# Gated delta rule: the inverse of the next pair of heads beside the recurrence of this one, TensorE in order of emission

## The chip, the cores and the metric

The kernel runs on one core of a Trainium2 chip. The metric is the device time in microseconds of one execution: 2815.87 us, the median of three runs (2814.72 to 2819.11).

## The reference

A chain of decoder blocks over 512 tokens of width 1024 in float32: a gated feed-forward, a block of parallel mixers, a cross attention, a feed-forward, a second block with retention and sparse attention, a third with neighbourhood and latent attention, a last feed-forward. The change lies in the parallel mixers of the first block, in one of the two mixers above all, the gated delta rule with 8 heads of 128, in chunks:

```python
m = jnp.where(strict, einsum(kb, kc) * decay, 0.0)        # per head and chunk
t_sys = eye + m
u = triangular_solve(t_sys, vb)
w = triangular_solve(t_sys, kb * exp(gc))
a_qk = einsum(qc, kc) * decay
def step(state, xs):                                      # over the chunks
    v_new = u_i - w_i @ state
    o_i = (q_i * exp(g_i)) @ state + a_i @ v_new
    state = state * exp(g_last) + k_dec.T @ v_new
```

q, k and v come from one projection each, a causal convolution of 4 taps and SiLU; q and k are normalised by their length. The result of a head is normalised, multiplied by SiLU of a projection z, and projected. The other mixer multiplies a projection by the sigmoid of another and convolves it with 31 taps.

## The kernel before

The kernel is written on a framework that tracks what each instruction needs, and that plans the order of every engine's instructions when the program is built: by a priority that falls in the order of emission, by what is ready, and by its own estimate of durations. `tc.high_priority(-n)` puts instructions n places later. The order that a queue then has is fixed; each engine takes its instructions in that order, and waits where one is not ready.

A projection of 128 features (`glu_conv`, `gdn_rows`, `gate_proj`, and the z product in `gdn_head`) loads a block of 1024 by 128 weights (`wload`, L273): one DMA of 512 KB in SyncE's queue (L277) into one of two raw buffers, a rounded copy `wh` by ScalarE (L270), the remainder `wl` by an engine named in `now["lo"]`, here GpSimd (L271). Then 24 products (`mm3`, L196, lines 198 to 200) of 128x512 add up in one PSUM bank of the group `pj`, which has three.

The gated delta rule uses chunks of 128 tokens, four to a head. For a head, `gdn_rows` (L692) makes k, q and v, takes the four taps (L716), turns them on TensorE (L726), squares them (L731), sums the rows (L734, L738), scales k (L740), and turns k back (L744). `gdn_decay` (L757) builds the decay, from a row that is loaded to all partitions, and the two score products of a chunk (L773) with their evictions (L776, L778); it stores one of them to `sm` in DRAM (L779). `gdn_blocks` (L783) inverts the 16x16 diagonal blocks of two heads at once on VectorE: it loads them (L790), does 15 steps of two dependent operations (L796, L798), stores the result and its transpose (L799, L802), and loads both back as Y and X (L804, L806). `gdn_head` (L814) completes the inverse from blocks of 16 to 128 by products in three levels (L822; eight steps), and then goes through the four chunks, three steps each (products with the state and the gating, L858; with the inverse, L866; with the new rows, L872). Each of these steps is one round of evictions by VectorE or ScalarE, after which comes the generator's `yield`. It ends with the norm, the z projection and the product with it (L886 to L910).

`glu_conv` (L561) makes two projections; ScalarE's sigmoid of one (L578) is multiplied with the other's bank by VectorE into `pad` (L579; two buffers), and 31 taps follow, the first on ScalarE, 30 on VectorE (L585), into the only bank of the group `cv`.

The stage is set together at L1821 to L1825: first a few projections; then two streams are emitted side by side by `interleave` (L212), which always advances the one with the smaller sum of estimated TensorE time (`pe_ns`, from `mm` and `mm3`) by its weight. The first holds the rows of heads 2 to 7, the convolutions and the `ga` gate; the second the pairs of heads, one after another, each as decay, blocks, heads (`gdn_pair`, L809). TensorE's order is the planner's.

Of the kernel before, what the change touches and what calls it, by code (L numbers as in the profile page):

```python
# [2 lines left out]

# [14 lines left out]
T = 512  # L18
# [7 lines left out]
CONV_LATER = 150  # L26
# [82 lines left out]
def kernel(ctx: ExitStack, tc: tile.TileContext, a: dict, out: bass.AP, upto=99):  # L109
# [9 lines left out]
    ypool = ctx.enter_context(tc.tile_pool(name="ypool", bufs=7))  # L119
# [9 lines left out]
    now = {"lo": V, ("sb", "wr"): (rpool, 2), ("sb", "wh"): (wpool, 4), ("sb", "wl"): (wpool, 4)}  # L129
# [94 lines left out]

# [48 lines left out]
    def wload(src, k0, kn, c0, cn, eng=None):  # L273
# [3 lines left out]
        S.dma_start(rv, src[k0 * 128:(k0 + kn) * 128, c0:c0 + cn].rearrange("(k p) c -> p k c", p=128))  # L277
# [32 lines left out]
    def feature_proj(src, c0, nf, act, nk, consume, tag="pj", group=2):  # L310

        f = 0
        while f < nf:
# [3 lines left out]
            for k0 in range(0, nk, step):  # L317
# [7 lines left out]
                yield  # L325
# [3 lines left out]
            yield  # L329
# [231 lines left out]
    def glu_conv(c0, c1):  # L561
        w = dram_w("w_in")
        act = acts["b1_1"]
        for c in range(c0, c1):
# [3 lines left out]
            for base in (4112, 4112 + 1024):  # L568
                p = bank()
                h, l = wload(w, 0, 8, base + c * 128, 128)  # L570
                for k in range(8):
                    mm3(p, (h[:, k], l[:, k]), (act.hi(k), act.lo(k)), k == 0, k == 7)
                ps.append(p)
                yield
            pad = work("pad", (128, T + 30))
            V.memset(pad[:, :30], 0.0)
            sg = work("sg", (128, T))
            A.activation(sg, ps[1], AF.Sigmoid)  # L578
            V.tensor_mul(pad[:, 30:], sg, ps[0])  # L579
# [6 lines left out]
            yield  # L586
# [40 lines left out]
    def gdn_gates():  # L627
# [7 lines left out]
        ab = work("sg", (128, T))  # L635
# [4 lines left out]
        small = work("gsmall", (128, 12, 32))  # L640
# [34 lines left out]
        V.tensor_tensor(small[:, 8], pc[:, 32:64], small[:, 5], OP.subtract)  # L675
        A.activation(small[:, 6], small[:, 5], AF.Exp)
        V.tensor_scalar(small[:, 7], small[:, 6], -1.0, None, OP.mult)
        V.tensor_scalar(small[:, 11], small[:, 5], -1.0, None, OP.mult)
        A.activation(small[:, 8], small[:, 8], AF.Exp)
        A.activation(small[:, 9], pc[:, 32:64], AF.Exp)  # L680
        gd.update(rq=sm(10), beta=sm(0), ngc=sm(11), egc=sm(6), negc=sm(7), kd=sm(8), egl=sm(9))
# [10 lines left out]
    def gdn_rows(h):  # L692
# [7 lines left out]
        for i in (1, 0, 2):  # L700
            if ("pre", h) in gd:
                p = gd["pre", h][i]
            else:
                hw, lw = wload(w, 0, 8, i * 1024 + h * 128, 128)
                p = bank()
                for k in range(8):
                    mm3(p, (hw[:, k], lw[:, k]), (act.hi(k), act.lo(k)), k == 0, k == 7)
            x = work("xr", (128, T))
# [14 lines left out]
            yield  # L723
            p = tbank()
            for c in range(4):
                PE.transpose(p[:, c], xf[:, c], ident)  # L726
            if i == 2:
                A.copy(v, p)
                break
            s_ = work("sq", (128, 4, 128))  # L730
            A.activation(s_, p, AF.Square)  # L731
            if i == 0:
                r = gd["rq"][:, :, h]
                V.reduce_sum(r, s_, axis=AX.X)  # L734
                inv_sqrt(r, r, 128.0, 128.0 * RMS_EPS, 4)
            else:
                r = tiny((128, 4))
                V.reduce_sum(r, s_, axis=AX.X)  # L738
                inv_sqrt(r, r, 1.0, RMS_EPS, 4)
                V.tensor_tensor(s_, p, r[:, :, None].to_broadcast([128, 4, 128]), OP.mult)  # L740
                yield
                p = tbank()
                for c in range(4):
                    PE.transpose(p[:, c], s_[:, c], ident)  # L744
                A.copy(kq[:, :, 0], p)
                G.tensor_tensor(kdec, s_, four(gd["kd"], h), OP.mult)
            yield
        gd["rows", h] = kq, v, kdec
        yield
# [7 lines left out]
    def gdn_decay(h):  # L757
        while ("rows", h) not in gd:
            yield
# [7 lines left out]
        mc, yx = slot(FT, (128, 2, 4, 128), "mc"), slot(FT, (128, 2, 4, 128), "yx")  # L767
        mt, at, Y, X = mc[:, 0], mc[:, 1], yx[:, 0], yx[:, 1]
        for cc in range(2):
# [8 lines left out]
            V.tensor_tensor(at[:, 2 * cc:2 * cc + 2], p[:, :, 1], dt_[:, 2 * cc:2 * cc + 2], OP.mult)  # L778
        S.dma_start(chunks(gd["sm"], h % 2), mt)  # L779
        gd["decay", h] = mt, Y, X, at  # L780
        yield

    def gdn_blocks(h):  # L783
# [5 lines left out]
        ub, yb, tb = work("ub", (64, 16, 16)), work("yb", (64, 16, 16)), work("tb", (64, 256))  # L789
        S.dma_start(ub, blocks(gd["sm"]))  # L790
        V.memset(yb, 0.0)
        V.memset(yb.rearrange("p a b -> p (a b)")[:, ::17], 1.0)
        yield
        for k in range(15, 0, -1):
            t = tb[:, :k * (16 - k)].rearrange("p (i j) -> p i j", i=k)
            V.tensor_tensor(t, ub[:, 0:k, k:k + 1].to_broadcast([64, k, 16 - k]),  # L796
                            yb[:, k:k + 1, k:16].to_broadcast([64, k, 16 - k]), OP.mult)
            V.tensor_tensor(yb[:, 0:k, k:16], yb[:, 0:k, k:16], t, OP.subtract)  # L798
        S.dma_start(blocks(gd["sy"]), yb)  # L799
        xb = work("tb", (64, 16, 16))  # L800
        A.copy(xb, yb.rearrange("p a b -> p b a"))
        S.dma_start(blocks(gd["sx"]), xb)  # L802
        for i in range(2):
            S.dma_start(gd["decay", h + i][1], chunks(gd["sy"], i))  # L804
        for i in range(2):
            S.dma_start(gd["decay", h + i][2], chunks(gd["sx"], i))  # L806
        yield

    def gdn_pair(h):  # L809
        yield from interleave((gdn_decay(h), 1.0), (gdn_decay(h + 1), 1.0))  # L810
        yield from gdn_blocks(h)
        yield from interleave((gdn_head(h), 1.0), (gdn_head(h + 1), 1.0))

    def gdn_head(h):  # L814
        kq, v, kdec = gd["rows", h]
        mt, Y, X, at = gd["decay", h]
# [5 lines left out]
        for n in (16, 32, 64):  # L822
            pairs = [(slice(0, 128), slice(0, 128))]
            if n > 16:
# [3 lines left out]
                for c in range(4):  # L828
                    PE.transpose(p[q, c, q], Y[q, c, q], ident[q, q])
                A.copy(X[q, :, q], p[q, :, q])  # L830
                yield
# [9 lines left out]
            yield  # L841
# [9 lines left out]
            yield  # L851
        o = t2((128, 4, 128))
        Sx = None
        for c in range(4):
# [9 lines left out]
            yield  # L864
# [4 lines left out]
            yield  # L869
# [15 lines left out]
            yield  # L885
        s_ = t2((128, 4, 128))  # L886
        A.activation(s_, o, AF.Square)
        r = tiny((128, 4))
        V.reduce_sum(r, s_, axis=AX.X)
# [6 lines left out]
        w = dram_w("w_in")  # L896
        act = acts["b1_1"]
        hw, lw = wload(w, 0, 8, 3072 + h * 128, 128)
        pz = bank()
        for k in range(8):  # L900
            mm3(pz, (hw[:, k], lw[:, k]), (act.hi(k), act.lo(k)), k == 0, k == 7)
        z = t2()
        A.activation(z, pz, AF.Silu)
        yield
        p = bank(tag="gt", shape=(128, 4, 128))
        for c in range(4):
            PE.transpose(p[:, c], o[:, c], ident)
# [4 lines left out]
        yield  # L912
# [890 lines left out]
    with ExitStack() as outer:  # L1803
        outer.enter_context(room(dict(ma=12)))
        mark("gdn")
        with room(kq=4, vk=3, mc=2, yx=2, pad=2, sg=1, xr=3, sq=2, t2=4, sqc=1, gsmall=1, ub=1, yb=1, tb=1):
            sq = work("sqc", (128, 5, 128))
            S.dma_start(sq, a["k_squares"][:, 1:6])
# [154 lines left out]
```

## Time and profile before

| what | value |
|---|---|
| median of three runs | 2815.87 us |
| the profiled execution | 2811.54 us, its span 2809.8 us |
| TensorE busy in the span | 2675.9 us (95%) |
| VectorE, ScalarE, GpSimd busy | 1384.9, 1042.5, 459.3 us |
| mean clock granted to TensorE | 0.981 |

Busy times are sums over the whole span, and say nothing on the stage of a stall. A matmul's length in the timeline holds the way through the array, so the spacing of two starts is shorter than the length that stands there: in a row of n equal ones, the length of the row less that of one, divided by n - 1, is the spacing. An idle time of TensorE is put down to what ended it.

### The profile page before, as it was taken

To read this page: it belongs to the slowest core of one execution; us is meant where nothing else is said; L and a number is where in the kernel's file an instruction comes from. 1 tells how busy PE (TensorE), PEld (TensorE's weight loads), DVE (VectorE), ACT (ScalarE), POOL (GpSimd) and SP (SyncE) were. 2 spreads that over 40 slices of the span, in tenths; PEclk is the share of its full clock that TensorE was granted. 3 is DMA by queue.
4 is the path that set the end of the run, shared out by engine and by line. 5 is a ranking of instruction groups with operands and counts; after the bars stand their busy time and mean duration, and the time that the engine had idled before them with its cause. 6 is when DMAs were issued, how large, how long until landed. Compare 5 with 4: busy or idle time off the path is not lost.

```text
span 2809.8 us, 34685 instructions
## 1 busy us (share of the span) xinstructions
PE 2675.9 (95%) x13600; PEld 2173.1 (77%) x13600; DVE 1384.9 (49%) x2516; ACT 1042.5 (37%) x1810; POOL 459.3 (16%) x325
## 2 busy tenths in 40 slices
PE   9999999887898999999999989999999999999998
PEld 7888877666676888888888867775787767888887
DVE  3232368874873356454233365575454464622324
ACT  4222235433344332433222254463256564222221
POOL 0101034333341011002101030131002001211011
PEclk9999999998899999999999999999999999999999
DMA  5323266357443433524223234312235122432322
GB/s 192 98 98 96 92 125 91 62 87 59 80 73 74 98 128 124 168 83 157 92 98 96 97 102 119 94 59 76 80 104 99 50 64 94 157 113 94 96 96 83
DMA packets 326035, 277.29 MB, mean 99 GB/s; under 512 B 50328, under 2 KB 278000, under 8 KB 325872
## 3 DMA queue, kind: packets, MB, share of 16 engines
q1 hardware_dynamic: 317808, 260.40, 35.6%
q10 hardware_dynamic: 8064, 14.68, 1.4%
q8 instruction: 107, 1.75, 0.3%
q14 instruction: 56, 0.46, 0.0%
HBM read 256.64 MB, written 20.49 MB: 99 GB/s over the span
## 4 chain that ended last, share of the span: by engine, by line
PE 47%; DVE 4%; POOL 1%; ACT 1%; issue 1%; DMA 1%; SPq 0%; DVEq 0%; ACTq 0%; POOLq 0%
PE mm L198 13%; PE mm L200 13%; PE mm L199 13%; PE mm L194 5%; DVE m L306 1%; PE mm L1595 1%; POOL t L955 0%; POOL hr L295 0%; DVE m L305 0%; PE mm L1353 0%; DVE wl L271 0%; DVE mf L306 0%; DVE st L433 0%; ACT wh L270 0%; DMA wr<-in_w_in 0%
## 5 line engine op out<-in xcount | busy, mean ns | idle before, releaser
L198 PE MATMUL mm<-x,wl 128*128 128x512 f32 (+3 forms) x2072 | 802.5, 387 | 31.4 <-DVE pad L579 25.4
L271 DVE TENSOR_TENSOR wl<-wr,wh 128x1024 fp32r<-128x1024 f32 (+1 forms) x351 | 427.0, 1217 | 799.7 <-ACT wh L270 798.6
L199 PE MATMUL mm<-x,wh 128*128 128x512 f32 (+3 forms) x2072 | 796.7, 385 | 0.0
L200 PE MATMUL mm<-x,wh 128*128 128x512 f32 (+3 forms) x2072 | 796.0, 384 | 0.0
L270 ACT CAST wh<-wr 128x1024 fp32r<-128x1024 f32 (+2 forms) x425 | 436.6, 1028 | 808.7 <-PE mm L200 518.9
L198 PEld LDWEIGHTS mm<-x,wl 128*128 128x128 f32 (+2 forms) x2072 | 395.2, 191 | 110.6 <-DVE pad L579 27.1
L200 PEld LDWEIGHTS mm<-x,wh 128*128 128x128 f32 (+2 forms) x2072 | 394.9, 191 | 75.2 <-issue 2.7
L199 PEld LDWEIGHTS mm<-x,wh 128*128 128x128 f32 (+2 forms) x2072 | 395.6, 191 | 72.1 <-issue 2.2
L271 POOL TENSOR_TENSOR wl<-wr,wh 128x1024 fp32r<-128x1024 f32 x74 | 177.3, 2399 | 491.8 <-ACT wh L270 485.2
L271 POOL TENSOR_TENSOR h<-t,h 128x512 fp32r<-128x512 f32 x66 | 101.7, 1541 | 837.0 <-ACT h L270 837.0
L200 PE MATMUL mm<-wh,h 128*128 128x512 f32 x528 | 205.6, 389 | 0.0
L198 PE MATMUL mm<-wh,h 128*128 128x512 f32 x528 | 205.5, 389 | 0.0
L199 PE MATMUL mm<-wl,h 128*128 128x512 f32 x528 | 205.5, 389 | 0.0
L585 DVE SCALAR_TENSOR_TENSOR mm<-pad,cols,mm 128x512 f32<-128x512 f32 x232 | 173.9, 749 | 11.6 <-ACT mm L583 9.1
L199 PEld LDWEIGHTS mm<-wl,h 128*128 128x128 f32 x528 | 99.1, 188 | 20.5
L200 PEld LDWEIGHTS mm<-wh,h 128*128 128x128 f32 x528 | 99.1, 188 | 20.5
L198 PEld LDWEIGHTS mm<-wh,h 128*128 128x128 f32 x528 | 99.1, 188 | 20.5
L490 ACT ACTIVATE t<-mm 128x512 f32<-128x512 f32 x66 | 39.5, 599 | 129.5 <-PE mm L200 129.5
L491 DVE SCALAR_TENSOR_TENSOR t<-t,mm 128x512 f32<-128x512 f32 x66 | 45.4, 688 | 78.6 <-POOL h L271 54.9
L198 PE MATMUL mm<-m,wl 128*128 128x512 f32 (+1 forms) x224 | 81.7, 365 | 0.0
L200 PE MATMUL mm<-m,wh 128*128 128x512 f32 (+1 forms) x224 | 81.1, 362 | 0.0
L199 PE MATMUL mm<-m,wh 128*128 128x512 f32 (+1 forms) x224 | 80.9, 361 | 0.0
(449 smaller groups left out, 3655.4 us busy)
## 6 DMA issues: line engine op xcount, KB each, us to landing
wr<-in_w_in SPq DMA_DIRECT2D x122, 512.0 KB
wr<-in_ffn_wg SPq DMA_DIRECT2D x44, 512.0 KB
wr<-in_ffn_wu SPq DMA_DIRECT2D x44, 512.0 KB
wr<-in_ffn_wd SPq DMA_DIRECT2D x44, 512.0 KB
wr<-in_w_ffn_in SPq DMA_DIRECT2D x44, 512.0 KB
wr<-in_w_ffn_out SPq DMA_DIRECT2D x22, 512.0 KB
xd<-m ACTq DMA_DIRECT2D x32, 256.0 KB
wr<-in_w_xkv SPq DMA_DIRECT2D x16, 512.0 KB
```

The costliest lines, as they stand in the source:

```text
L194: PE.matmul(o, lhsT, rhs, start=start, stop=stop)
L198: PE.matmul(o, lh[1], rh[0], start=start, stop=False)
L199: PE.matmul(o, lh[0], rh[1], start=False, stop=False)
L200: PE.matmul(o, lh[0], rh[0], start=False, stop=stop)
L270: A.copy(hi, src)
L271: (eng or V).tensor_sub(lo, src, hi.bitcast(FT))
L306: V.scalar_tensor_tensor(yh, yh, r, bh, OP.mult, OP.add)
L490: A.activation(sg, ps[0][f], AF.Silu)
L491: V.scalar_tensor_tensor(sg, sg, scale, ps[1][f], OP.mult, OP.mult)
L585: V.scalar_tensor_tensor(s_ if j < 30 else o, pad[:, j:j + T], tap31(j, c), s_, OP.mult, OP.add)
L1595: PE.transpose(p[:, kt], Ps[hp][:, kt * 128:(kt + 1) * 128], ident)
```

## The change

The inverse of a pair (`gdn_decay`, `gdn_blocks`) leaves `gdn_pair` and becomes `gdn_ahead`. `gdn_heads` advances the two heads of a pair and the `gdn_ahead` of the next pair by a step each. `phase` emits such a chain and, after each step, projections worth `share` ns of estimated TensorE time; what is left of the projections comes after the chain. `after` puts work off until so much TensorE time has been emitted: the turning of q, k and v comes 8 us after their projection, the turning back of k another 8 us later. After the rows of head 0, each product and transpose on TensorE is tied to the one emitted before it. The z projection becomes one of the fillers (`gdn_z`, the same lines as before, with a `yield` after every six products). `now["dq"]` is ScalarE through the stage, so the weights' DMAs are issued from its queue.

Beside these: the 31 taps rank 300 places later (150 before), the blocks' VectorE operations 100; the gate goes by a copy on ScalarE and a product on GpSimd; the squares of rows are summed by ScalarE, chunk by chunk; GpSimd scales k, from a copy in SBUF; k and q lie in the group `ma`; `vk` has six buffers in place of three; the small tiles `t1` six in place of seven. `mm` counts 230 ns in place of 300, `mm3` 680 in place of 650, in all interleavings of the kernel.

```diff
...
-CONV_LATER = 150
+CONV_LATER = 300
+BLOCKS_LATER = 100
...
-    ypool = ctx.enter_context(tc.tile_pool(name="ypool", bufs=7))
+    ypool = ctx.enter_context(tc.tile_pool(name="ypool", bufs=6))
...
+    order = {"on": False, "last": None}
+
+    def placed(inst):
+
+        if order["on"]:
+            if order["last"] is not None:
+                tc.add_manual_dep(inst.ins, order["last"].name, mybir.DependencyInfo(
+                    mybir.DependencyClass.NoSync, mybir.DependencyReason.DATA), reason="order of emission")
+            order["last"] = inst.ins
+
+    def in_order(on):
+        order.update(on=on, last=None)
+
...
     def mm(o, lhsT, rhs, start=True, stop=True):
-        pe_ns[0] += 300.0
-        PE.matmul(o, lhsT, rhs, start=start, stop=stop)
+        pe_ns[0] += 230.0
+        placed(PE.matmul(o, lhsT, rhs, start=start, stop=stop))
 
     def mm3(o, lh, rh, start, stop):
-        pe_ns[0] += 650.0
-        PE.matmul(o, lh[1], rh[0], start=start, stop=False)
-        PE.matmul(o, lh[0], rh[1], start=False, stop=False)
-        PE.matmul(o, lh[0], rh[0], start=False, stop=stop)
+        pe_ns[0] += 680.0
+        placed(PE.matmul(o, lh[1], rh[0], start=start, stop=False))
+        placed(PE.matmul(o, lh[0], rh[1], start=False, stop=False))
+        placed(PE.matmul(o, lh[0], rh[0], start=False, stop=stop))
+
+    def turn(o, x, i):
+        pe_ns[0] += 110.0
+        placed(PE.transpose(o, x, i))
...
+    later = []
+
+    def after(ns, work_):
+        later.append((pe_ns[0] + ns, work_))
+
+    def due(all_=False):
+
+        for i, (t, work_) in enumerate(later):
+            if all_ or t <= pe_ns[0]:
+                del later[i]
+                work_()
+                return True
+        return False
+
+    def phase(chain, filler, share):
+
+        filler, credit = iter(filler), 0.0
+
+        def fill():
+            before = pe_ns[0]
+            if not due() and next(filler, None) is None:
+                return None
+            return pe_ns[0] - before + 20.0
+
+        for _ in chain:
+            credit += share
+            while credit > 0:
+                took = fill()
+                if took is None:
+                    break
+                credit -= took
+        while fill() is not None:
+            pass
...
-        S.dma_start(rv, src[k0 * 128:(k0 + kn) * 128, c0:c0 + cn].rearrange("(k p) c -> p k c", p=128))
+        now["dq"].dma_start(rv, src[k0 * 128:(k0 + kn) * 128, c0:c0 + cn].rearrange("(k p) c -> p k c", p=128))
...
+            A.copy(pad[:, 30:], ps[0])
+            sg = work("xr", (128, T))
             A.activation(sg, ps[1], AF.Sigmoid)
-            V.tensor_mul(pad[:, 30:], sg, ps[0])
+            G.tensor_tensor(pad[:, 30:], pad[:, 30:], sg, OP.mult)
...
-        kq = slot(FT, (128, 4, 2, 128), "kq")
+        kq = slot(FT, (128, 4, 2, 128), "ma")
...
+        def squares(r, x):
+            for c in range(4):
+                A.activation(t1(), x[:, c], AF.Square, accum_out=r[:, c:c + 1])
...
+        def of_k(x):
+            p = four_turned(x)
+            s_ = work("sq", (128, 4, 128))
+            A.copy(s_, p)
+            r = tiny((128, 4))
+            squares(r, s_)
+            inv_sqrt(r, r, 1.0, RMS_EPS, 4)
+            G.tensor_tensor(s_, s_, r[:, :, None].to_broadcast([128, 4, 128]), OP.mult)
+
+            def back():
+                A.copy(kq[:, :, 0], four_turned(s_))
+                G.tensor_tensor(kdec, s_, four(gd["kd"], h), OP.mult)
+                ready()
+
+            after(8000.0, back)
+
+        for i, then in ((1, of_k), (0, of_q), (2, of_v)):
...
+            after(8000.0, lambda then=then, xf=xf: then(xf))
+            yield 1
...
+        with tc.high_priority(-BLOCKS_LATER):
+            V.memset(yb, 0.0)
+            V.memset(yb.rearrange("p a b -> p (a b)")[:, ::17], 1.0)
+            for k in range(15, 0, -1):
+                t = tb[:, :k * (16 - k)].rearrange("p (i j) -> p i j", i=k)
+                V.tensor_tensor(t, ub[:, 0:k, k:k + 1].to_broadcast([64, k, 16 - k]),
+                                yb[:, k:k + 1, k:16].to_broadcast([64, k, 16 - k]), OP.mult)
+                V.tensor_tensor(yb[:, 0:k, k:16], yb[:, 0:k, k:16], t, OP.subtract)
...
+    def gdn_ahead(h):
+
         yield from interleave((gdn_decay(h), 1.0), (gdn_decay(h + 1), 1.0))
         yield from gdn_blocks(h)
-        yield from interleave((gdn_head(h), 1.0), (gdn_head(h + 1), 1.0))
+
+    def gdn_heads(h, ahead):
+        live = [gdn_head(h), gdn_head(h + 1)]
+        while live:
+            live = [g for g in live if next(g, None) is not None]
+            next(ahead, None)
+            yield 1
...
+            A.activation(t1(), o[:, c], AF.Square, accum_out=r[:, c:c + 1])
...
+        while ("z", h) not in gd:
+            yield 1
+        z = gd["z", h]
...
+        with room(vk=6, mt=4, at=4, Y=4, X=2, pad=2, xr=3, sq=1, t2=4, sqc=1, gsmall=1, ub=1, yb=1, tb=1):
...
-            if True:
-                run(glu_conv(0, 1), gdn_rows(1), glu_conv(1, 2))
-                proj = seq(*[g for h in range(2, 8) for g in (gdn_rows(h), glu_conv(h, h + 1))],
-                           gate_proj("ga", "w_in", 6160, acts["b1_1"], None, "ma"))
-                chains = seq(*[gdn_pair(h) for h in (0, 2, 4, 6)])
-                run(interleave((proj, 1.2), (chains, 1.0)))
-            now["lo"] = V
+            now["dq"] = A
+            in_order(True)
+            ga = gate_proj("ga", "w_in", 6160, acts["b1_1"], None, "ma")
+            phase((), seq(glu_conv(0, 1), gdn_rows(1), glu_conv(1, 2)), 0.0)
+            phase(gdn_ahead(0), seq(gdn_rows(2), gdn_rows(3), glu_conv(2, 3)), 1500.0)
+            phase(gdn_heads(0, gdn_ahead(2)), seq(gdn_rows(4), gdn_rows(5), glu_conv(3, 4), gdn_z(0), gdn_z(1)), 3000.0)
+            phase(gdn_heads(2, gdn_ahead(4)), seq(gdn_rows(6), gdn_rows(7), glu_conv(4, 5), gdn_z(2), gdn_z(3)), 3000.0)
+            phase(gdn_heads(4, gdn_ahead(6)), seq(glu_conv(5, 7), gdn_z(4), gdn_z(5), islice(ga, 5)), 2000.0)
+            phase(gdn_heads(6, iter(())), seq(glu_conv(7, 8), gdn_z(6), gdn_z(7), islice(ga, 5)), 1500.0)
+            in_order(False)
+            run(ga)
+            now.update(lo=V, dq=S)
...
```

## Rows read from the trace of the kernel before

**Rows 1.** page part 2, the span in 40 slices: TensorE busy, clock granted.
```profile
PE   9999999887898999999999989999999999999998
PEclk9999999998899999999999999999999999999999
```

**Rows 2.** table of stretches: us; busy (count) PE, PEld, DVE, ACT, POOL; clock; DMA; GB/s.
```profile
100.00:200.00 100.00, 100.00 (x443) 82.81 (x442) 28.07 (x27) 24.69 (x29) 9.29 (x6) 1.00 0.30 100
386.00:905.00 519.00, 442.69 (x2494) 360.82 (x2494) 352.10 (x709) 214.19 (x381) 177.10 (x101) 0.92 0.52 80
...
499.00:514.00 15.00, 6.57 (x18) 5.00 (x19) 14.38 (x33) 3.91 (x5) 1.11 (x2) 0.54 0.52 114
...
854.00:869.00 15.00, 4.43 (x23) 4.46 (x24) 1.33 (x2) 1.04 (x1) 2.34 (x1) 0.54 0.68 150
```

**Rows 3.** what TensorE waited for, 386 to 905: us, times, longest.
```profile
PE mm L198 <- DVE pad L579: 25.4, 4, 11.9
PE mm L194 <- DVE mc L778: 20.0, 3, 12.2
PE mm L194 <- DMA yx<-sx: 12.8, 2, 12.0
PE mm L744 <- DVE sq L740: 9.0, 3, 5.0
```

**Rows 4.** timeline, first and last pair's inverse, SyncE's issues and VectorE's first use of X.
```profile
465.98 2.39 SPq L779 DMA_DIRECT2D sm<-mc  x2
...
472.78 0.69 SPq L790 DMA_DIRECT2D ub<-sm  x1
...
506.15 0.62 SPq L799 DMA_DIRECT2D sy<-yb  x1
...
509.70 1.05 SPq L806 DMA_DIRECT2D yx<-sx  x2
...
515.21 0.69 DVE L837 TENSOR_TENSOR yx<-mm,sqc 128x512 f32<-128x512 f32 x1 [1.67 <-PE mm L194]
...
822.58 2.75 SPq L779 DMA_DIRECT2D sm<-mc  x2
...
866.66 0.69 DVE L837 TENSOR_TENSOR yx<-mm,sqc 128x512 f32<-128x512 f32 x1 [18.20 <-PE mm L194]
```

**Rows 5.** what SyncE's queue waited for, 386 to 905: us, times, longest.
```profile
SPq L277 <- POOL wl L271: 292.4, 50, 19.7
```

**Rows 6.** timeline of TensorE: start, length, instructions of a chain in one row.
```profile
460.95 2.75 PE L194 MATMUL mm<-kq 128*128 128x256 f32 x12
...
885.16 1.15 PE L194 MATMUL mm<-t,kq 128*128 128x128 f32 x8
```

**Rows 7.** groups of instructions by line and shape, 386 to 905: busy us, mean ns.
```profile
L198 PE MATMUL mm<-x,wl 128*128 128x512 f32 x424 | 179.2, 423 | 29.2 <-DVE pad L579 25.4 <-ACT sg L578 2.3 <-DVE yb L798 1.4
...
L585 DVE SCALAR_TENSOR_TENSOR mm<-pad,cols,mm 128x512 f32<-128x512 f32 x232 | 173.9, 749 | 11.6 <-ACT mm L583 9.1
...
L766 ACT ACTIVATE t<-t,gsmall 128x128 f32<-128x128 f32 x32 | 10.1, 390 | 27.5 <-POOL t L764 27.5
...
L746 POOL TENSOR_TENSOR vk<-sq,gsmall 128x512 f32<-128x512 f32 x8 | 8.4, 1051 | 13.6 <-DVE yb L798 7.2 <-ACT gsmall L680 5.3 <-DVE sq L740 0.8
...
L740 DVE TENSOR_TENSOR sq<-mm,tiny 128x512 f32<-128x512 f32 x8 | 5.5, 692 | 3.1 <-POOL tiny L295 3.1
```

**Rows 8.** timeline: one DMA issue in ScalarE's queue, one weight load in SyncE's.
```profile
381.03 0.33 ACTq L428 DMA_DIRECT2D xd<-m  x1
...
482.20 0.37 SPq L277 DMA_DIRECT2D wr<-in_w_in  x1
```

**Rows 9.** timeline of GpSimd and VectorE in the block inverse.
```profile
478.72 0.18 DVE L796 TENSOR_TENSOR tb<-ub,yb 64x39 f32<-64x39 f32 x1
...
479.77 2.40 POOL L271 TENSOR_TENSOR wl<-wr,wh 128x1024 fp32r<-128x1024 f32 x1 [4.08 <-ACT wh L270]
480.29 1.95 DVE L796 TENSOR_TENSOR tb<-ub,yb 64x48 f32<-64x48 f32 x1
```

More of the change, by code (lines that the diff above doesn't have):

```diff
@@ L2 @@
 from contextlib import ExitStack
+from itertools import islice
 import numpy as np
@@ L639, in gdn_gates @@
             PE.transpose(pt[:, tt, :16], ab[:16, tt * 128:(tt + 1) * 128], ident[:16, :16])
-        small = work("gsmall", (128, 12, 32))
+        small = work("gsmall", (128, 8, 32))
         def sm(i):
@@ L722, in gdn_rows @@
                 A.activation(x, x, AF.Silu)
[L723 to L749, printed above, removed]
+            after(8000.0, lambda then=then, xf=xf: then(xf))
+            yield 1
     def chunks(t, i):
@@ L758, in gdn_decay @@
         while ("rows", h) not in gd:
-            yield
+            yield 1
         kq, v, kdec = gd["rows", h]
@@ L810, in gdn_pair @@
+        S.dma_start(blocks(gd["sy"]), yb)
+        A.copy(ub, yb.rearrange("p a b -> p b a"))
+        S.dma_start(blocks(gd["sx"]), ub)
+        for t, s_ in (("Y", "sy"), ("X", "sx")):
+            for i in range(2):
+                m = work(t, (128, 4, 128))
+                S.dma_start(m, chunks(gd[s_], i))
+                gd["decay", h + i].append(m)
+        yield 1
+    def gdn_ahead(h):
         yield from interleave((gdn_decay(h), 1.0), (gdn_decay(h + 1), 1.0))
         yield from gdn_blocks(h)
-        yield from interleave((gdn_head(h), 1.0), (gdn_head(h + 1), 1.0))
+    def gdn_heads(h, ahead):
[3 more added lines that the diff above has]
+            next(ahead, None)
+            yield 1
+        for _ in ahead:
+            yield 1
@@ L895, in gdn_head @@
         G.tensor_tensor(o, o, r[:, :, None].to_broadcast([128, 4, 128]), OP.mult)
[L896 to L904, printed above, removed]
+        while ("z", h) not in gd:
+            yield 1
+        z = gd["z", h]
         p = bank(tag="gt", shape=(128, 4, 128))
         for c in range(4):
-            PE.transpose(p[:, c], o[:, c], ident)
+            turn(p[:, c], o[:, c], ident)
         if h // 2 not in gd:
@@ L911, in gdn_head, with gdn_z @@
                                OP.mult, OP.mult)
-        yield
+        yield 1
+    def gdn_z(h):
+        w = dram_w("w_in")
+        act = acts["b1_1"]
+        hw, lw = wload(w, 0, 8, 3072 + h * 128, 128)
+        p = bank()
+        for k in range(8):
+            mm3(p, (hw[:, k], lw[:, k]), (act.hi(k), act.lo(k)), k == 0, k == 7)
+            if k % 2:
+                yield 1
+        z = t2()
+        A.activation(z, p, AF.Silu)
+        gd["z", h] = z
+        yield 1
     def gate_proj(key, wname, c0, act, bias, tag="m", bt="pj", group=2):
@@ L1805 @@
         mark("gdn")
-        with room(kq=4, vk=3, mc=2, yx=2, pad=2, sg=1, xr=3, sq=2, t2=4, sqc=1, gsmall=1, ub=1, yb=1, tb=1):
-            sq = work("sqc", (128, 5, 128))
-            S.dma_start(sq, a["k_squares"][:, 1:6])
-            triu, gneg, ones, lev = sq[:, 0], sq[:, 1], sq[:, 2], sq[:, 3:5]
+        with room(vk=6, mt=4, at=4, Y=4, X=2, pad=2, xr=3, sq=1, t2=4, sqc=1, gsmall=1, ub=1, yb=1, tb=1):
+            sq, lev = work("xr", (128, 3, 128)), work("sqc", (128, 2, 128))
+            S.dma_start(sq, a["k_squares"][:, 1:4])
+            for i, j in enumerate((2, 4)):
+                S.dma_start(lev[:, i], a["k_squares"][:, j])
+            triu, ones, gneg, lev = sq[:, 0], sq[:, 2], lev[:, 0], lev[:, 1:2]
             zero = work("sq", (128, 4, 128))
```

99 lines of the change are left out of this document (51 added, 48 removed).

## The prediction

> **What bounds the kernel now.** I read the page's slices first: TensorE is at nine tenths almost everywhere, except in slices 8 to 13 (of 70 us each, counted from one), where it falls to seven and eight tenths, and in two of them its granted clock falls too [rows 1]. That is the stage of the gated delta rule, 386 to 905 us. The table of stretches gives it 519 us, with TensorE busy for 442.7, so idle for 76.3; VectorE is busy for 352.1, ScalarE for 214.2, GpSimd for 177.1 [rows 2]. No engine is full: the stage waits. The mean granted clock is 0.92; eight short stretches hold nearly all the time at the lower level (1.2 GHz). In them TensorE is busy for 43.3 us (sum over the eight; the first and the last stand in the rows), and each follows an idle time or holds it. At 2.4 GHz that work would take about 20 us less.
>
> The list of waits names the idle time: 25.4 us for VectorE's gate product into `pad`, 20.0 for the eviction of the two score products (L778), 12.8 for the DMA that brings X back, 9.0 for VectorE's scaling of k [rows 3]. Together 67.2 of 76.3. All are one pattern: a product stands in TensorE's queue ahead of projections that could run, and what it needs comes late.
>
> Two causes lie behind. The inverse of the 16x16 blocks is a long trip off TensorE: from the last store of `sm` to the first use of X it is 468.4 to 515.2 us for the first pair and 825.3 to 866.7 for the last, 47 and 41 us; the two pairs between take 48 and 53 [rows 4]. About 17 us of the first trip are DMA, about 30 are VectorE's. And SyncE issues in order: its weight loads wait 292.4 us for GpSimd to free the raw buffer [rows 5], and the chain's own small transfers stand behind them.
>
> **The parts of the change.** *Projections as filler.* One block of weights is 24 products. In a pure stretch 443 products take 100 us [rows 2], 0.226 each, so a block is 5.4 us. For a pair's chain: products over one chunk cost (1.15 - 0.28) / 7 = 0.12 us each, the 256-wide ones (2.75 - 0.42) / 11 = 0.21 [rows 6]. A pair has 100 of the first kind, 16 of the second, and small blocks and transposes, some 20 us; the transposes of the rows of two heads add 3.5. The 1272 wide projections of the stage (three lines with the count of L198 [rows 7]) are 287 us, some 110 half-wide ones 13, four pairs 94, the gates and the rest 9: 403 us at full clock and closest spacing. TensorE's 442.7 less the 20 of the clock is 423, so 20 us more lie in short turns between the two kinds. Nothing above 519 - 403 = 116 us can be won in the stage.
>
> *The waits that go.* The linear half of the gate is now copied to `pad` by ScalarE and multiplied by GpSimd in place, so neither bank hangs on VectorE: 25.4 us off. The score products of a pair are emitted eight chain steps into the pair before, with one or more steps between product and use: 20.0 off. The turning of k waits a further 8 us of emitted TensorE work: 9.0 off. The present X wait, 12.8, goes too and is put anew below. Sum -67.2. What is late next is X.
>
> *X, anew.* The next pair's score products end about eight chain steps into a phase, and the phase must last until X is back. Heads 0/1 and 2/3: ten blocks (six of rows, two of the convolution, two of z), 54 us, plus 24 of chain gives 78; the eighth step is at 24 of filler + 8 of the inverse's upper levels + 3.4 of scores, 35, which leaves 43. Heads 4/5: eight blocks (four of the convolution, two of z, two of the gate `ga`), 43, plus 20 gives 63; eighth step at 16 + 11.6 = 28, leaves 35. The lead-in for heads 0/1: eight blocks and the chain's 7, 50; eighth step at 15, leaves 35. The trip is 41 to 53 us. With SyncE free of weights I take 45, a little under the middle; it then comes late by 2, 2, 10 and 10, 24 us in all. Bounds: at 35 (17 of DMA and 18 of VectorE, as near as the last pair comes) nothing is late; at 55 it is 64.
>
> *New waits.* TensorE now takes its work strictly as emitted, so a step whose eviction is late holds everything behind it. There are some 88 steps (22 for each pair), with 1.5 to 3 us of projections between them against an eviction of 0.35 to 0.7. I take 0.1 each, 9 us; bounds 0 and 35.
>
> *Moves that I cost at nothing.* VectorE loses the gate product, the scaling of k, and three row sums for each head, 40 operations at about 0.69 (L740 [rows 7]), 27.5 us: cover for the rest. GpSimd gets eight scalings and eight gate products, 1.05 each as L746 [rows 7], 17 us on 177. ScalarE gets 96 squares of one chunk at 0.39 (the nearest is L766 [rows 7]), at most 37 us, 10 of copies, and 56 weight issues at 0.33 to 0.37 [rows 8], 20 us: 214 becomes at most 281, and a stage of 465 covers it. If that cover is gone, rival three says what it costs. The fewer small buffers (six for seven) and the changed weights of the interleaving elsewhere I take at 0, +-6: outside the stage TensorE stays nearly full [rows 1].
>
> *The Trainium skill, "DMA: Bandwidth & Descriptors", section "Issuing engines are not separate DMA queues"*, says that starting DMAs from several engines saves only the sequencer's time, as all end on the same 16 DMA engines. The trace has the DMA engines at 0.52 over the stage [rows 2], so there is room; but by that rule the trip keeps its mean of 47, lateness is 32, and the sum below would be 8 us smaller.
>
> **The sum.** Idle: -67.2 + 24 + 9 = -34. Clock: of the 20 us, two late X's of 10 us keep a low stretch each, about the 4 to 5 us that such a stretch costs now (43.3 / 8 / 2 = 2.7, more after a long idle): -11. Turns between kinds: projections now come in runs of six or more, half of the 20 is won: -9 (0 to -20). Together -54. The profiled execution took 2811.54 us (span 2809.8 and 1.7 around it), so 2757.5; the median of the runs is 4.3 higher. I forecast 2815.9 - 54 = 2762. With the terms' bounds the likeliest case reaches from -25 to -80: 2736 to 2791.
>
> **Rivals.** *One: everything is hidden.* Without weights in SyncE's queue and with VectorE 27.5 us lighter, the trip falls to 35. For it: the last pair, with few convolution taps about, is already at 41. Against: the taps (232 at 0.75 [rows 7]) still have to go somewhere. Then -67 + 5 of idle, -18 of clock, -15 of turns, -95: 2721.
>
> *Two: VectorE's block inverse gets longer.* Its 30 dependent operations now rank behind the other work, and GpSimd has 17 us more. The trace shows what GpSimd does to them: such an operation takes 0.18 us at 478.72, and 1.95 at 480.29 while GpSimd's subtraction runs from 479.77 to 482.17 [rows 9]. If every pair's trip grows by 10 us over my 45, lateness is 64 in place of 24, and the low clock takes 6 more: -54 + 46 = -8, 2808. The Trainium skill, "SBUF — State Buffer", section "Who interferes with whom", says that a VectorE instruction with two SBUF inputs and a GpSimd instruction that reads SBUF block each other for a whole instruction; by it, GpSimd's new products too lengthen this inverse, and the trace's 1.95 us agrees.
>
> *Three, slower: ScalarE blocked by its weight issues.* The 292.4 us that SyncE waits for GpSimd could land on ScalarE, whose queue also holds the evictions of the chain and the casts of the weights. At full size 281 + 292 = 573 us of ScalarE bind a stage of 519: +54, 2870. It decides from about 240 us of such waiting. Against it: SyncE waits because it has nothing else to do; the order within ScalarE's queue is planned at build time, and an issue can be put behind the casts and evictions that are ready sooner. Nothing in the trace shows the price of that plan being wrong.
>
> *Four: the gate does not come free.* That is, this part does not do what it says. There are still two `pad` buffers and one bank for the taps; if the copy into `pad` waits for an earlier channel's taps, the 25.4 us stay, with some clock: -54 + 30 = -24, 2792.
>
> **Chances.** Likeliest 0.45, everything hidden 0.25, long inverse 0.15, ScalarE 0.10, `pad` 0.05. A measurement of this kernel tells about 0.2%, 5.6 us, from no change. Long inverse is split: half of it faster, the rest the same or a little slower. So faster 0.82, same 0.06, slower 0.12. The range holds the likeliest case, most of the first rival and the better part of the second: 2710 to 2806, which leaves out little more than ScalarE's case and the tails.
>
> **What would show it.** In the profile after: weight loads under ScalarE's queue, and SyncE's small ones close behind their inputs. TensorE's waits for `pad`, the score evictions and the scaled k gone or near it; its longest waits at the starts of pairs, for X, two near 10 us and two near 2. Granted clock of the stage at 0.95 or more. VectorE at some 325 us within a stage of about 465. I am wrong if the list has many short waits for ScalarE or VectorE in the recurrence (then emission order costs more than 0.1 a step), if ScalarE idles on GpSimd's subtraction for more than 100 us, or if waits for X pass 50.

## The result, and the profile after

The changed kernel is slower. It takes 2840.28 us (median of four runs, 2835.66 to 2843.28) against 2816.9 for the kernel before on the same chip: ratio 1.0082, 95% interval 1.0063 to 1.0100. I had forecast 2762 with a range of 2710 to 2806. The profiled execution took 2842.67 us, its span 2840.9.

The loss is in the stage of the gated delta rule. The first weights of `w_gdn_out`, the next projection, were asked for at 924.3 us before and are at 962.6 now: 38.3 us later, while the span grew by 31.1. So the rest of the kernel won 7 us (every version of the changed kernel below takes 1877 to 1882 us from there to the end, the kernel before 1885.5), and the stretch that answers to 386 to 905 is now 386 to 943.3. First the table of stretches (columns as in [rows 2]), with 15 us that matter below; then the two lines of the page that answer to [rows 1].

```profile
386.00:943.30 557.30, 447.16 (x2495) 367.45 (x2495) 341.20 (x677) 244.24 (x575) 193.60 (x117) 0.89 0.49 74
853.00:868.00 15.00, 3.35 (x20) 3.06 (x19) 11.74 (x16) 3.41 (x4) 2.35 (x1) 0.69 0.18 35
```

```profile
PE   9999986788788999999999999999999999999998
...
PEclk9999998899899999999999999999999999999999
```

TensorE is idle for 557.3 - 447.2 = 110.1 us, before 519 - 442.7 = 76.3 [rows 2]: +33.8. Where the granted clock is at its lower level (1.2 GHz), TensorE is busy for 65.2 us in fourteen stretches, before for 45.3 in ten (the prediction's 43.3 are eight of these, in windows that were a little wide). A wide product starts 0.43 us after the one before it there, 0.23 elsewhere, so about half of the difference is the clock's, +10. The rest of the busy time, by the same estimate, is what it would be at 2.4 GHz: 414.5 for 420.0, -5.5. Together +38.3. What TensorE waited for, after (us, times, longest; answers to [rows 3]):

```profile
PE mm L218 <- POOL t L982: 23.8, 8, 8.7
PE mm L218 <- ACT ma L821: 20.3, 1, 20.3
PE mm L208 <- issue: 19.3, 2, 11.6
PE mm L208 <- DVE t L948: 9.9, 3, 3.8
PE mm L218 <- ACT t L770: 8.0, 2, 5.8
PE mm L208 <- DMA X<-sx: 7.7, 1, 7.7
PE mm L208 <- DVE at L856: 6.0, 2, 5.3
PE mm L208 <- ACT t L956: 4.9, 4, 3.4
PE mm L218 <- ACT xr L824: 2.8, 3, 1.1
```

The four lines of [rows 3], 67.2 us, have shrunk to 13.7: no wait for `pad`, none for the scaled k, 6.0 for the score evictions, 7.7 for X. In their place stand waits that the kernel before hardly had: GpSimd's norm at the end of each head (L982), one SiLU of q (L821), the evictions and row sums of small steps (L948, L956, L770), the SiLU of k or v (L824), and 19.3 us under "issue", which the profile can't name. Without X and the scores these seven lines are 89.0 us. What the list leaves out is 7.7 us, about what the kernel before had beside its four lines (9.1).

The line marked issue is two places, and their cause can be read from the timelines. This is TensorE at the start of the fourth pair: eight products with X for the first head, then 11.65 us of nothing, then those for the second head.

```profile
853.51 1.05 PE L208 MATMUL mm<-X,mt 128*128 128x128 f32 x8
866.21 1.19 PE L208 MATMUL mm<-X,mt 128*128 128x128 f32 x4 [11.65 <-issue]
```

X is not late there: SyncE issued its loads at 847.70. VectorE in the same time:

```profile
855.21 9.46 DVE L640 SCALAR_TENSOR_TENSOR mm<-pad,cols,mm 128x512 f32<-128x512 f32 x12
864.70 0.75 DVE L640 SCALAR_TENSOR_TENSOR ma<-pad,cols,mm 128x512 f32<-128x512 f32 x1
865.36 1.40 DVE L991 SCALAR_TENSOR_TENSOR ma<-mm,cols,t 128x512 f32<-128x512 f32 x2
```

L991 is the multiply that reads the turned output of the two heads just finished, out of PSUM. The tag `gt` has three banks: two hold these outputs, the third took the first head's product, so the second head's product needs one that L991 must empty. L991 stands behind thirteen taps of the convolution, and the first of its two ends, at 866.11, stands 0.10 us before TensorE's next start. The other place, 762.9 to 770.6, looks the same (seven taps and the last tap ahead of L991).

ScalarE now issues the weights, and its idle time names something new. Idle time put down to GpSimd's subtraction `wl` is 85.2 us in 27 places (the sum of fifteen lines of its waits; none before). The issue of a load waits until GpSimd has freed the raw buffer, and what is next in ScalarE's queue waits with it. One of the 27 (ScalarE; the subtraction runs from 646.44 to 648.81):

```profile
645.31 1.05 ACT L323 CAST wh<-wr 128x1024 fp32r<-128x1024 f32 x1 [0.30 <-DMA wr<-in_w_in]
648.85 0.37 ACTq L330 DMA_DIRECT2D wr<-in_w_in  x1
649.27 0.60 ACT L1005 ACTIVATE t<-mm 128x512 f32<-128x512 f32 x1 [2.90 <-POOL wl L324]
649.76 0.30 ACT L976 ACTIVATE t<-t 128x128 f32<-128x128 f32 x1
649.96 0.19 ACT L976 ACTIVATION_READ_ACCUMULATOR t<-t 128x1 f32 x1
```

L976 is the square of the norm at a head's end, one for each chunk. The third of this head starts at 644.61, the fourth only at 649.76, behind the issue; TensorE stands for this norm from 647.9 to 656.5. In the same 8.7 us VectorE's last small product of the norm, 128x4, takes 2.29 us in place of some 0.16, while GpSimd subtracts:

```profile
653.06 2.29 DVE L981 TENSOR_TENSOR tiny<-tiny,gsmall 128x4 f32<-128x4 f32 x1 [0.45 <-POOL tiny L348]
653.00 2.34 POOL L324 TENSOR_TENSOR wl<-wr,wh 128x1024 fp32r<-128x1024 f32 x1
```

The longest single wait, 20.3 us for the SiLU of q (L821), is a place in a queue too. VectorE's last products of a four-tap convolution (L818) before it end at 447.90, so its input is there. ScalarE has it behind casts that wait for their weights, an issue that waits for `wl`, and eight exponentials (L843):

```profile
445.59 2.31 DVE L818 SCALAR_TENSOR_TENSOR xr<-mm,cols,xr 128x511 f32<-128x511 f32 x3
457.71 1.04 ACT L323 CAST wh<-wr 128x1024 fp32r<-128x1024 f32 x1 [4.30 <-DMA wr<-in_w_in]
461.21 0.37 ACTq L330 DMA_DIRECT2D wr<-in_w_in  x1
461.61 1.28 ACT L843 ACT_TABLE_LOAD   x1 [2.17 <-POOL wl L324]
466.65 0.63 ACT L821 ACTIVATE ma<-xr 128x512 f32<-128x512 f32 x1
```

### The profile page after: what moved, and what is told of

Its sections match the earlier page's. It is cut to its first block, busy times and chain, and to the rows that moved or that the text cites. A ratio compares the mean times of both kernels' runs of the same rounds, so it can differ in the third digit from the quotient of the medians.

```text
span 2840.9 us, 34780 instructions
## 1 busy us (share of the span) xinstructions
PE 2678.6 (94%) x13600; PEld 2180.7 (77%) x13600; DVE 1368.0 (48%) x2476; ACT 1062.1 (37%) x1993; POOL 473.1 (17%) x341
## 4 chain that ended last, share of the span: by engine, by line
PE 46%; DVE 4%; POOL 1%; issue 1%; DMA 1%; ACT 1%; DVEq 0%; ACTq 0%; POOLq 0%; SPq 0%
PE mm L212 13%; PE mm L213 13%; PE mm L214 13%; PE mm L208 6%; DMA wr<-in_w_in 1%; DVE m L359 1%; DVE wl L324 1%; PE mm L1690 0%; POOL hr L348 0%; POOL t L1050 0%; ACT wh L323 0%; DVE m L358 0%; PE mm L1448 0%; PE mm L1740 0%; DVE mf L359 0%
```

## The experiments

Each kernel is compared with the kernel before on the same chip; ratios, with 95% intervals, are used between different sets. "Fixed" means TensorE in the order of emission, "free" without it.

**Which part of the change costs.** Two parts were undone in the changed kernel, each alone and both, and one was done alone in the kernel before.

```
# e1, e4
-            now["dq"] = A
+            now["dq"] = S
# e3, e4
-            in_order(True)
# e2, in the kernel before
-        S.dma_start(rv, src[k0 * 128:(k0 + kn) * 128, c0:c0 + cn]...
+        now.get("dq", S).dma_start(rv, src[k0 * 128:(k0 + kn) * 128, c0:c0 + cn]...
...
+            now["dq"] = A          # ahead of the stage's projections
```

e1, fixed order, SyncE issues:

> The changed kernel, with the stage's weight DMAs issued by SyncE again. Theory A (issue): in the changed kernel ScalarE waits 85 us at 27 places for GpSimd to free a raw buffer, because a weight DMA stands in its queue; evictions and casts behind it are late and TensorE, in order of emission, holds. Then this version loses most of that: TensorE's idle time in the stage falls from 110 to 60 us or less, 2780 us. Theory B (order of emission): the end of a pair (23.8 us for the norm) and the late X (27 us) cost the time whoever issues; then 2830 to 2840 us.

e2:

> The kernel before, with the stage's weight DMAs issued by ScalarE and nothing else changed. Theory A: ScalarE waits some 80 us for GpSimd and the time rises by 20 to 40 us, to 2837 to 2857. Theory B: within 6 us of before, 2811 to 2823.

e3, free order, ScalarE issues:

> The changed kernel without the ties between TensorE's instructions: the planner orders them, weights still issued by ScalarE. Theory A: the late evictions stay, the planner could not know of them; 2825 to 2845. Theory B: the end of a pair and X no longer hold the projections; 2790 to 2805.

e4, free order, SyncE issues:

> Both undone: TensorE's order is the planner's and SyncE issues the weights; the emission beside each other, the gate on GpSimd and the row sums on ScalarE stay. Theory A: like the version with SyncE's issue alone, 2770 to 2785. Theory B: like the version with the free order alone, 2790 to 2805. If both cost, below either, 2750 to 2765.

| | ScalarE issues | SyncE issues |
|---|---|---|
| fixed order | 1.0082 [1.0063, 1.0100] (the change) | 1.0069 [1.0048, 1.0089], 2831.42 us |
| free order | 0.9975 [0.9964, 0.9987], 2807.65 us | 0.9873 [0.9857, 0.9890], 2777.75 us |
| kernel before | 1.0013 [0.9995, 1.0031], 2816.21 us | 1 |

e1 and e2 came as theory B said, e3 lay 3 us above its range, and e4 fell in theory A's range although e1 and e2 had spoken against A: neither theory holds alone, and the two parts do not add up. The fixed order costs 30 us (0.0107 of 2815) with ScalarE's issues and 55 with SyncE's. ScalarE's issues cost 29 us in the free order; in the fixed order and in the kernel before nothing that can be told apart, although the latter's ScalarE too idled on `wl` for 52.1 us in 20 places. The amount of such waiting does not tell its price: in e3, where the issues cost 29 us, it is 41.0 us in 17 places. The long wait for q's SiLU shows the same: 20.3 us in the changed kernel, 14.9 in e1, 18.8 in e3, and 1.7 in e4; of these four it goes only where both parts are undone. What is left of the change, e4, wins 1.27%: it beats both kernels. Its stage and its waits:

```profile
386.00:879.20 493.20, 438.67 (x2496) 357.94 (x2495) 342.50 (x678) 243.05 (x573) 193.92 (x117) 0.95 0.54 84
```

```profile
PE mm L218 <- POOL t L982: 14.3, 6, 3.3
PE mm L218 <- ACT xr L824: 8.0, 2, 7.7
PE mm L212 <- DVE xr L818: 4.7, 1, 4.7
PE mm L208 <- ACT X L918: 4.0, 1, 4.0
PE mm L208 <- issue: 3.7, 1, 3.7
```

**Two hold points? (a theory that fell).** I took X at the pairs' starts and the norm at their ends for the places that hold the fixed order. f5 runs the inverse two steps for each step of the recurrence; f6 puts a head's last transposes off by 8 us of emitted work; f7 has both with SyncE's issues, f8 both with SyncE's issues and the free order.

```
# f5, in gdn_heads
             next(ahead, None)
+            next(ahead, None)
# f6, at the end of gdn_head
+        def end():
+            if ("z", h) not in gd:
+                after(1000.0, end)
+                return
...
+        after(8000.0, end)
```

> The changed kernel, in which the next pair's inverse advances two steps for each step of this pair, so that its score products are emitted some four steps earlier (about 12 us). Theory C: the order of emission costs what its hold points cost, and X is one of them (27 us in three waits at the starts of pairs, two of them listed as issue); then these waits fall under 8 us in all and the time to about 2812 us. Rival D: the order costs at every late eviction, so the wait that goes turns up at the next ones; 2830 us or more.

> The changed kernel, in which the last transposes of a head (after its norm) are put off by 8 us of emitted TensorE work, so that they come beside the next pair or the remaining projections. Theory C: the 24 us that TensorE waits for GpSimd's scaled result at the ends of pairs go, with some clock; about 2815 us. Rival D: 2830 us or more.

> Order of emission kept; weights issued by SyncE, the inverse two steps at a time, the ends of heads put off. Theory C: the three effects add up, 2831 less some 50, 2780 us, near the version with the planner's order and SyncE's issue (2778). Rival D: 2805 us or more, since in the fixed order each late eviction still stops the projections.

> The version with the planner's order and SyncE's issue (2778 us), with the inverse two steps at a time and the ends of heads put off. It still waits some 14 us for the scaled results and 8 us for X. Theory C, as far as the planner's order leaves hold points: 2760 to 2770 us. Rival: the planner has placed these already, 2773 to 2783.

f5: 2842.24 us, 1.0105 [1.0090, 1.0120]. For the last pair X's loads go out 23.5 us sooner (824.18 for 847.70), and TensorE's list still has the same entry:

```profile
PE mm L208 <- issue: 19.3, 2, 11.6
```

So these waits were never for X, and this sent me to VectorE's queue. f6: 2836.48, 1.0082 [1.0065, 1.0098]; the waits for the norm and those under issue went and others came, the largest of them, 22.5 us in two lines, for L991, which has line 993 there:

```profile
PE mm L208 <- DMA X<-sx: 15.2, 2, 8.2
PE mm L218 <- DVE ma L993: 15.1, 2, 13.5
PE mm L208 <- DVE t L948: 13.1, 3, 5.5
...
PE mm L208 <- DVE ma L993: 7.4, 1, 7.4
```

It is the multiply described above, again behind taps: its first run starts at 768.66, after thirteen of them. f7: 2821.07, 1.0026 [1.0008, 1.0043]: with SyncE's issues the two edits gain 12 us on e1, not the 50 of theory C. f8: 2785.79, 0.9904 [0.9890, 0.9919], no better than e4, and above both of its expectations. In f5, f6 and f7 the time came out as rival D said.

**The multiply behind the taps.** L991 and the last tap of a channel write buffers of one kind (`ma`), and at both places L991's buffer is asked for right after the one that this tap is the first to write. In the build L991 then comes right after that tap. The edit, called the claim below, writes one column of the convolution's buffer early, so that it is taken before:

```
             if c % 2 == 0:
                 cv.setdefault("out", []).append(slot(FT, tag="ma"))
+                V.memset(cv["out"][-1][:, 0, :1], 0.0)      # h1, h3: only if c >= 4
```

g3 is the changed kernel with it, g5 has SyncE's issues too, g4 is e4 with it. g6 is g5 with 15 of the 30 taps left out.

> The changed kernel with one 128x1 memset per second convolution channel, which claims the convolution's output buffer early. Theory E: at the start of the third and the fourth pair the second head's first product with X waits for a PSUM bank that holds the last head's turned output; the multiply that empties it stands in VectorE's queue right behind the last tap of the convolution (13 taps and more), because both write buffers of one kind and these are granted in the order asked for. With the claim the multiply goes ahead of the taps: the waits of 7.7 and 11.7 us marked issue go, the run falls by 13 to 20 us to about 2823. Rival D (in a fixed order a wait that goes turns up at the next late eviction, as the runs with the inverse two steps ahead and with the later end showed): the two waits go, but the run is 2833 or more.

> The same with the weights issued by SyncE: beside the run of the changed kernel with SyncE's issues (2831, ratio 1.0069), which has the same two waits of 9.3 and 11.6 us. Theory E: about 2814, no different from the kernel before. Rival D: 2825 or more.

> The claim in the kernel without the fixed order and with SyncE's issues (2777.75, the fastest so far). There the same two places cost 4.0 and 3.7 us of idle TensorE, since other products can go first. Both theories: 2770 to 2778.

> As the run with the claim and SyncE's issues, with 15 of the 30 taps of the convolution on VectorE left out: some 95 us less of VectorE's work, none of TensorE's. Theory F: most of what is left of the fixed order's cost is the chain's small VectorE steps standing behind taps of 0.75 us; then the end of the pairs (20 us of waits for the norm) and the waits for VectorE fall by 15 us or more, and the run to 2800 or less. Rival: the waits left come from ScalarE's evictions and GpSimd's norm, and the run stays within 6 us of the one with all taps.

g3: 2809.05 us, 0.9983 [0.9973, 0.9992], 28 us less than the change by the ratios; four small memsets turn the slower kernel into one that is 0.17% faster than before. Theory E had expected 13 to 20. g5: 2797.38, 0.9944 [0.9927, 0.9960]. g5 too went 17 us below theory E's 2814. g4: 2788.2, 0.9911 [0.9896, 0.9926], 11 us slower than e4, a miss for both theories. g6: 2778.88, 0.9876 [0.9859, 0.9894], 19 us less than g5. That is as much as theory F asked for, but not where it looked: g5's largest wait, for the first X, went, and the norm's stayed. The waits of g5, then of g6:

```profile
PE mm L208 <- DMA X<-sx: 22.2, 1, 22.2
PE mm L218 <- POOL t L983: 20.0, 8, 6.5
PE mm L218 <- ACT sq L788: 9.7, 1, 9.7
```

```profile
PE mm L218 <- POOL t L983: 23.9, 8, 8.0
PE mm L218 <- ACT sq L788: 8.2, 1, 8.2
```

So the taps hold the first block inverse, whose 30 small steps stand among them one by one in g5's VectorE queue; the waits for the norm do not fall with the taps' number.

Open after this: which of the four claims pays, whether the kernel before would have gained as much, and the price of the first X.

> The changed kernel with the claim for the last two of the four buffers only (those of channels 4 and 6, which stand ahead of the two late multiplies). Theory E1 (these two waits and what they bring with them are the claim's worth): nothing changes ahead of 740 us, the two waits go, about 2820. Theory E2 (all four buffers held something up, at the start of the stage too): the wait of 20.3 us at 447 us stays, and the run stays 10 us or more above that with all four claims (2809).

> The kernel before with the same claim. If the held multiply is a cost of the changed kernel's order: within 5 us of 2814. If the old kernel paid it too: 10 us or more faster.

> The claim for the last two buffers in the kernel without the fixed order and with SyncE's issues (2777.75; with all four claims 2788). Theory E: the two waits of 3.7 and 4.0 us go, about 2772. If claims change the order of the free kernel's work at random: between 2775 and 2790.

> The kernel with the fixed order, SyncE's issues and the claim (2797), with the z projections of the first two heads (some 11 us of TensorE) moved from the first pair's recurrence ahead of it, where TensorE waits 22 us for the first X. Theory F (that wait is open on the path): 8 to 11 us faster, about 2787. Rival D: the first recurrence then lacks this work between its steps and loses as much, 2793 to 2800.

h1, the changed kernel with the last two claims alone: 2820.78 us, 1.0016 [1.0005, 1.0026]. That is E1's 2820, but also more than 10 us above g3, as E2 said: the expectations did not part the two. VectorE at the start of the fourth pair (L991 is L993 here, L925 is L927), then TensorE:

```profile
838.81 0.75 DVE L642 SCALAR_TENSOR_TENSOR mm<-pad,cols,mm 128x512 f32<-128x512 f32 x1
839.47 0.74 DVE L993 SCALAR_TENSOR_TENSOR ma<-mm,cols,t 128x512 f32<-128x512 f32 x1
840.77 0.75 DVE L993 SCALAR_TENSOR_TENSOR ma<-mm,cols,t 128x512 f32<-128x512 f32 x1 [0.55 <-PE mm L218]
841.43 3.12 DVE L642 SCALAR_TENSOR_TENSOR mm<-pad,cols,mm 128x512 f32<-128x512 f32 x4
844.46 0.68 DVE L927 TENSOR_TENSOR X<-mm,sqc 128x512 f32<-128x512 f32 x1
```

```profile
843.35 1.95 PE L208 MATMUL mm<-X,mt 128*128 128x128 f32 x16
```

The multiplies go at most one tap after the transposes are there, and the sixteen products of the two heads run in one piece. The two waits (19.3 us) are gone, and the run is 18.6 us shorter by the ratios. The start's wait of 20.3 us stays (20.7), as both said. The first two claims are worth another 9 us (g3 against h1), a third of the whole: there the wait of 20.3 goes, and the first wait for X grows from 7.8 to 19.4. Why they change the start was not followed up.

h2, the kernel before with the claims: 2815.89, 1.0007 [0.9996, 1.0018], no change. The cost belongs to the changed kernel. h3, e4 with the last two claims: 2783.56, 0.9890 [0.9872, 0.9908], no gain on 0.9873, where theory E had 2772. h4: 2792.62, 0.9924 [0.9909, 0.9939]; the wait for the first X falls from 22.2 to 12.2 us, 5.6 us less than g5 by the ratios with intervals that overlap, so F and D are not told apart.

Why the free order doesn't mind is seen in e4 at the same place. There L991 is held about as long: twelve taps, and L991 at 810.05.

```profile
800.69 8.66 DVE L640 SCALAR_TENSOR_TENSOR mm<-pad,cols,mm 128x512 f32<-128x512 f32 x11
809.38 0.75 DVE L640 SCALAR_TENSOR_TENSOR ma<-pad,cols,mm 128x512 f32<-128x512 f32 x1
810.05 1.40 DVE L991 SCALAR_TENSOR_TENSOR ma<-mm,cols,t 128x512 f32<-128x512 f32 x2
```

TensorE, however, has projections ahead of the second head's products in its queue, and stands for 3.67 us in place of 11.65:

```profile
806.61 0.39 PE L213 MATMUL mm<-x,wh 128*128 128x512 f32 x1
806.84 0.39 PE L214 MATMUL mm<-x,wh 128*128 128x512 f32 x1
810.90 1.48 PE L208 MATMUL mm<-X,mt 128*128 128x128 f32 x6 [3.67 <-issue]
```

With the held multiply (and what else the claims moved) out of the way the price of the fixed order with SyncE's issues falls from 55 us (e1 against e4) to 9 (g5 against g4). Of these 46 us, 35 are won in the fixed order and 11 are lost in the free one; against e4, the fastest of all, the best fixed versions, h4 and g5, are still 14 and 20 us slower.

## Why the prediction was wrong

**The step that failed** is "New waits": 88 steps at 0.1 us, 9 us in all, bounds 0 and 35. It measured 89.0. I priced what a late eviction of a normal step costs in a fixed order, with projections of 1.5 to 3 us between steps. What happened is that few places hold everything: 11.6 and 7.7 us at the two held multiplies, where no projection is emitted between the first products of the two heads, 20.3 at one SiLU at the start, eight ends of heads with 23.8 together. The average was the wrong measure, and "an eviction of 0.35 to 0.7" was the wrong duration: the eviction is short, its place in VectorE's or ScalarE's queue is not. Shown by h1 for two of these places: undoing them alone takes back 18.6 of the 23 us between the two kernels. For the SiLU and the ends of heads the queue is read from the timeline, and no run prices them alone.

The profile came out 85 us above the prediction's sum (2842.7 for 2757.5): the new waits lie about 79 us above their term, the clock 21, the score evictions 6 and the turns 3.5; X lies 16 us below its term, and the rest of the kernel 7.

**The waits that go** (-67.2): right. 61.2 of it went, taking X's line out of the count as the prediction does; the scores keep 6.0.

**X anew** (+24: 2, 2, 10, 10): too large. One wait of 7.7 us is put down to X, for the first pair. From the end of the last stores of `sm` to the issue of X's loads it is 45, 25, 23 and 46 us for the four pairs (502.97 to 547.80, 598.06 to 622.61, 699.75 to 722.58, 801.70 to 847.70 in SyncE's queue; before, by the same measure, 41, 43, 48 and 31), where I had 45 to X's use for each: the two in the middle are back long before they are wanted, and the first and the last grew. Freeing SyncE of the weights is not what did it: in e1, where SyncE issues them again, the four are 46, 24, 21 and 41. The Trainium skill, "DMA: Bandwidth & Descriptors", section "Issuing engines are not separate DMA queues", says that issuing from several engines saves only the sequencer's time; these two rows agree. What the prediction hung on it, a trip of 47 and X late by 32, did not come: the wait was 7.7 us, and what shortened the two middle trips was not followed up.

**The clock** (-11): wrong in sign, +10; the idle time grew by 33.8 us in place of falling, and the low stretches went from ten to fourteen. **The turns between kinds** (-9): -5.5, right in kind, though read only as what the clock leaves of the busy time. **Outside the stage** (0 +-6): -7.

**Moves at nothing.** VectorE did fall, 352.1 to 341.2 where I had 325; ScalarE rose to 244.2 where I had at most 281. But that a stage of 465 covers ScalarE's work, the weight issues with it, counts busy time, and the cost is waiting. Rival three named this mechanism and set its point of decision at 240 us of waiting; 85.2 us were enough to be on the path of the norm and of q's SiLU. Its price, by the runs: 29 us in the free order, 11 with the claim (g3 against g5), not to be told from nothing in the fixed order as it came (there other waits may end later; that was not shown). So the sign came out as in that rival, but not by it: undone alone (e1) it leaves a kernel that is still slower. The other rivals did not happen: the waits for `pad` went (four), X was not late by more (two; though the last pair's inverse did get longer, 46 us for 31, as above), and little was hidden (one).

The signs that I named for being wrong were half right. There are waits for ScalarE and VectorE in the recurrence (L948, L956: 14.8 us in seven), but the decisive ones are long and at the seams between pairs. The two thresholds, 100 us of ScalarE on the subtraction and 50 of X, were not reached.

Not settled: what the claims of the first two buffers change at the start; why g4 is slower than e4; what the norm at the end of heads costs by itself (18.4 to 24.6 us of waits in the fixed versions but f6 and f7, which put it off; 14.3 in e4 and 9.2 in g4).

## What to carry to other kernels

When an engine is tied to the order of emission, do not price an average step: list the places where nothing independent is emitted between a product and the bank or tile that it needs, and for each look at what stands ahead of the releasing instruction in its own engine's queue. A wait that the profile can't name may be for a PSUM bank: find the reader of the bank's last contents, and see what it stands behind. Buffers of one kind that are asked for by two chains can tie these chains together. Where an engine issues transfers that wait for a buffer, everything behind the issue waits too; here that cost 29 and 11 us in two of four comparisons and nothing that could be told apart in the other two. Such issues are safer on an engine without evictions.

## What the hardware showed that I had not expected

A square with a row sum on ScalarE is two instructions, ACTIVATE of 0.30 us and ACTIVATION_READ_ACCUMULATOR of 0.19, but the next square starts 0.29 us after the one before (649.76, 650.05), so a chunk costs 0.29 and not the 0.39 that I took. And a TensorE idle stretch of 11.65 us reads "issue" though it has a cause: the profile shows no releaser for it, and the cause had to be found from the other engines' timelines. In f6 the profile names the same multiply, for waits of 13.5 and 7.4 us.
